# Three experts with 64 slots loaded ahead of the routing, and 32 slots for the 14 emptiest

## The chip, the cores and the metric

The kernel runs on one core of a Trainium2 chip. The metric is device time in microseconds, as the median of the runs shown; a run is one launch of the whole layer. TensorE (PE) does the matrix products, VectorE (DVE) and ScalarE (ACT) the elementwise work, GpSimd (POOL) issues the gathers and scatters, and SyncE (SP) issues nearly all other transfers. Transfers of SP go through one queue in the order in which SP issues them, and SP waits in that order too.

## The reference

One residual layer on 512 tokens of 1024 channels, float32. First a mixer: a norm, one projection, a gated convolution branch and a spatial gating branch, and an output projection. Then a mixture of 32 experts in 4 groups, of which this change speaks:

```python
g_sel = jnp.argmax(g_logits, axis=-1)                      # one group of 4 for each token
e_logits = jnp.take_along_axis(e_logits, g_sel[:, None, None], axis=1)[:, 0]
top_v, top_i = lax.top_k(e_logits, TOP_K)                  # two of its 8 experts
e_w = jax.nn.softmax(top_v, axis=-1) * g_w
expert_id = g_sel[:, None] * EXPERTS_PER_GROUP + top_i
...
def run_block(args):                                       # SwiGLU, 1024 -> 512 -> 1024
    xb, e = args
    return (jax.nn.silu(xb @ w_gate[e]) * (xb @ w_up[e])) @ w_down[e]
...
y = y_pad[dest] * sorted_w[:, None].astype(h.dtype)
out = jnp.zeros((n_tok, d), h.dtype).at[sorted_tok].add(y)
```

A final norm follows. 512 tokens with two experts each make 1024 assignments over 32 experts. How they fall depends on the data. With the inputs of the reference (seed 0), experts 0, 1 and 2 get 16, 22 and 10 of them. The other 29, sorted by their counts, get 115, 113, 97, 88, 58, 55, 51, 36, 36, 32, 32, 31, 27, 26, 26, 20, 18, 16, 16, 15, 15, 11, 10, 10, 9, 4, 3, 3, 3.

## The kernel before

The mixer takes the first 457 us or so. It is split matmul work with its own weights, and it holds the on-chip memory that the experts' weights need afterwards. The router's logits are made token block by token block with the last matmuls of the mixer (`out_mm`, `out_tr`, `out_logits`, `route_norm`, `route_sel`, `route_rank`, `route_tab`), and the normed tokens are written to `h2d` in HBM by POOL (`h2_out`).

**Ranks.** After the last block the experts are sorted by their number of tokens, on the chip (`krow`, `kcol`, `kr`, `Pm`), and the sorted list of expert numbers, `eid`, is what SP reads to know which weights to load. The first `NS` places are an exception: they are experts 0 to `NS`-1 by number, whatever their counts (`kre` and `kce` hold the offsets that put them first). Since their numbers are known, their weights can be loaded before the routing is done.

**Slots.** Each rank has a fixed number of token slots: 128 for ranks below `NBIG`, 64 for those above. A last check (`capr`, `over`) compares the counts with the slots; if one does not fit, the branch `overflow` runs at the end and does the rest in `NOV` more blocks. With 128 slots an expert's gate and up products go to two PSUM tiles; with 64 slots they share one, gate in partitions 64 to 127 and up in 0 to 63, as column halves of the PE array.

**Order.** `order` lists the ranks as they are computed: the `NS` first, then as the string `ORDER` says (`s` the next of 64 slots, `b` the next of 128). Position n in that order is what the loops count.

**Weights.** An expert has three pieces of 2 MB: two of gate and up (`(n, 0)` and `(n, 1)`) and one of down (`(n, 2)`). The list `loads` is the order in which they go through SP's queue. `piece()` issues the next one. It goes to one of nine buffers (`SLOTS`, tags w0 to w8, taken in turn from `rot`) and waits for three things: that the buffer's last reader is done, that the load two places earlier has landed (`throttle`, `DEEP` is 2), and, from rank `NS` on, for `eid`. Loads are counted from 0 in what follows; loads 0 to 3·`NS`-1 are those of the experts that come first by number. Near the end of the list stand the last expert but one, then the two halves `Y` of the scattered results `yd` (2 MB each), then the three pieces of the last expert. The buffers lie where the mixer's tiles lay, so the first ones come free only as the mixer ends.

**One position n of the loop**, in PE's order: gate and up products with the two pieces (`up`), the transposes of the next position's tokens (`x_tr`, which also issues the gather of position n+4), the down products of position n-1 (`down`), the transposes of this position's hidden values (`h_tr`). `glu` on ACT and DVE lies between. `down` copies its result to `ysb` and POOL scatters it to `yd` by an indirect transfer; each scatter waits for the one before it to land, and what POOL has to do after it waits too. With 64 slots a token's row of 1024 is scattered as two half rows, from partitions 0 to 63 and 64 to 127. A gather moves `cap[r]` rows and a scatter of 64 slots `64 + cap[r]`, where `cap` also takes the bound 1024 / (r - NS + 1) on how many tokens rank r can hold, so the late ranks' transfers have numbers of rows such as 53, 46 or 37.

**The end.** The last three positions are not scattered but added on the chip (`late_down`, `late_add`, `late_x`). The `Y` loads read `yd`, so they wait for the last scatter, that of position 28. Then the rows are summed, normed and written, and the last expert's rows go out through one indirect transfer.

Of the kernel before, what the change touches and what calls it, by code (L numbers as in the profile page):

```python
# [8 lines left out]
F32 = mybir.dt.float32  # L9
FR = mybir.dt.float32r  # L10
I32 = mybir.dt.int32
F16 = mybir.dt.float16
# [9 lines left out]
NS, NBIG, DEEP, NLATE, LATE_AT = 2, 8, 2, 3, -16  # L22
NOV = 9
# [3 lines left out]
ORDER = "ssb" * 6 + "s" * 12  # L27
# [54 lines left out]
def body(tc, nc, d, out, dbg=None):  # L82
# [116 lines left out]
    pool.memset(capr[:, :NBIG], 128.0)  # L199
    pool.memset(capr[:, NBIG:], 64.0)  # L200
# [536 lines left out]
    cap = [128] * NS + [min(128 if r < NBIG else 64, 2 * T // (r - NS + 1)) for r in range(NS, NE)]  # L737
    order, bs_, ss_ = list(range(NS)), list(range(NS, NBIG)), list(range(NBIG, NE))
    for c in ORDER:
        order.append((bs_ if c == "b" else ss_).pop(0))  # L740
# [94 lines left out]
    def slots(p, n, gi_, si_):  # L835
# [21 lines left out]
    slots(tab[:, :NS], NS, gi[:, :NS], si[:, :NS])  # L857
# [39 lines left out]
    def x_tr(n):  # L897
        if n >= NE:
            return
        m = 128 if order[n] < NBIG else 64  # L900
        xg = XG[n % len(XG)]
        XT[n] = xT = m1.tile([128, KT, m], F32, name="xT", tag=("xh", "xl")[n % 2])
        nb = m * KT // 512
        kb = KT // nb
        for hf in range(nb):
            p = aux()
            for k in range(kb):
                kk = hf * kb + k
                pe.transpose(p[:, k * m:(k + 1) * m], xg[:m, kk * 128:(kk + 1) * 128], ident[:m, :m])  # L909
            pv = p.rearrange("p (k t) -> p k t", k=kb)  # L910
            ks = slice(hf * kb, hf * kb + kb)
            dve.tensor_tensor(xT[:, ks], pv, bc(gfp[:, ks], m), ALU.mult)
        gather(n + len(XG))

    def up(n, c):
        small = order[n] >= NBIG
        if c == 0:
            E[n] = {}
            p = acc()
            E[n]["g"], E[n]["u"] = (p[64:128], p[:64]) if small else (p, acc())  # L920
        w = W[n, c].rearrange("p (q k f) -> p q k f", q=2, k=4)
        for kk in range(4):
            kt = c * 4 + kk
            for q in range(2):
                pe.matmul(E[n]["gu"[q]], XT[n][:, kt], w[:, q, kk], start=kt == 0, stop=kt == KT - 1,  # L925
                          skip_group_check=True)

    def glu(n):
        m = 128 if order[n] < NBIG else 64
        s_ = m2.tile([128, DE], F32, name="sg", tag="sg")[:m]  # L930
        act.activation(s_, E[n]["g"], AF.Silu)  # L931
        E[n]["h"] = h = m2.tile([128, DE], F32, name="h", tag="h")[:m]
# [5 lines left out]
    def h_tr(n):  # L938
        m = 128 if order[n] < NBIG else 64
        p = acc()  # L940
        for k in range(4):
            pe.transpose(p[:, k * m:(k + 1) * m], E[n]["h"][:, k * 128:(k + 1) * 128], ident[:m, :m])
        hh = m2.tile([128, 4, m], F32, name="hh", tag="hh")
        act.activation(hh, p[:, :4 * m].rearrange("p (k t) -> p k t", k=4), AF.Copy)
# [10 lines left out]

    def down(n):
        small = order[n] >= NBIG
# [186 lines left out]
    def overflow():  # L1144
# [20 lines left out]
        dve.tensor_scalar(ce, ce, 64.0, None, ALU.add)  # L1165
# [130 lines left out]
```

## Time and profile before

| | |
|---|---|
| median of 3 runs | 1016.41 us (1015.29 to 1018.13) |
| the profiled execution | 1016.92 us, its span 1015.1 us |
| mean granted clock of PE | 0.973 |
| PE busy | 945.5 us, 93% of the span |
| DVE, ACT, POOL busy | 395.1, 225.7, 112.5 us |
| read from HBM, written | 260.06 MB, 17.97 MB |
| last matmul of the mixer | starts 454.17 us and runs in a group of 12 for 3.02 us |
| first matmul of an expert | 480.77 us |
| last weights issued | 984.9 us |

The rest of the profile is given by time from the span's start. A row of the timeline has the start, the duration, the engine, the line, the operation, the tiles that it writes and reads, how many such instructions in a row, and in brackets how long the engine sat idle before it and what ended that. `SPq` rows are issues of transfers: they last 0.33 us where they stand alone, and one row with several has the time from the first issue to the end of the last. A matmul of float32 is two instructions in the trace, so the 16 products of `up(n, c)` with 128 slots show as 16 instructions for 8 in the program.

### The profile page before, as it was taken

Reading aid. Unit: us, or ns where it says so; the run is one execution under the profiler, and the core shown is the slowest. Engines: PE = TensorE matmul, PEld = TensorE weight load, DVE = VectorE, ACT = ScalarE, POOL = GpSimd, SP = SyncE. Lnnn points to the kernel's source line nnn. Section 1 sums busy time; section 2 is a strip of 40 time slices with the busy share of each in tenths; the row PEclk is TensorE's granted clock in tenths of the full one; section 3 lists DMA queues with packets and bytes.
Section 4 is the critical chain, followed back from the end, with each engine's and each line's share of the span. In section 5 each row is a group of like instructions: output and inputs, shape, how many; then the busy total and the mean of one; then the engine's idle time right before and its main releaser. Section 6 shows DMA issues by size and latency. Waiting matters only on the chain. (4 is left out here: it accounts for less than half of the span.)

```text
span 1015.1 us, 10676 instructions
## 1 busy us (share of the span) xinstructions
PE 945.5 (93%) x4210; PEld 558.4 (55%) x4210; DVE 395.1 (39%) x662; ACT 225.7 (22%) x317; POOL 112.5 (11%) x102
## 2 busy tenths in 40 slices
PE   8999999999999999993999999999999998787774
PEld 6867588888778888883444443434444333232221
DVE  7697758889447534247111101110111111022053
ACT  6302223433237323232100101111100010110123
POOL 3300000000000000503011111111101021111010
PEclk9999999999999999996999999999999999999978
DMA  5558312322221333953989999999999999999794
GB/s 221 193 156 291 116 55 83 111 80 88 96 83 41 130 119 105 414 206 145 355 323 409 409 411 412 415 405 405 418 404 398 390 394 374 408 410 410 298 355 154
DMA packets 42536, 271.38 MB, mean 267 GB/s; under 512 B 12776, under 2 KB 15976, under 8 KB 25970
## 3 DMA queue, kind: packets, MB, share of 16 engines
q1 hardware_dynamic: 31680, 260.14, 65.8%
q0 software_dynamic: 10800, 10.51, 3.1%
q8 instruction: 35, 0.57, 0.2%
q14 instruction: 19, 0.16, 0.0%
q10 hardware_dynamic: 2, 0.00, 0.0%
HBM read 260.06 MB, written 17.97 MB: 274 GB/s over the span
## 5 line engine op out<-in xcount | busy, mean ns | idle before, releaser
L925 PE MATMUL acc<-w,xT 128*64 128x512 f32 (+1 forms) x1024 | 291.0, 609 | 18.0 <-DMA w<-in_wexp 18.0
L350 PE MATMUL acc<-hT,hl 128*128 128x512 f32 x912 | 210.5, 390 | 0.0
L925 PEld LDWEIGHTS acc<-w,xT 128*64 128x64 f32 (+1 forms) x1024 | 103.7, 153 | 182.4 <-issue 163.2
L350 PEld LDWEIGHTS acc<-hT,hl 128*128 128x128 f32 x912 | 170.7, 188 | 37.4 <-issue 1.9
L936 DVE TENSOR_TENSOR h<-sg,acc 64x512 f32<-64x512 f32 (+1 forms) x31 | 21.1, 681 | 364.8 <-ACT sg L931 252.3
L953 PE MATMUL acc<-w,hh 128*64 128x512 f32 (+1 forms) x512 | 146.3, 604 | 8.9 <-DMA w<-in_wexp 6.0
L156 DVE TENSOR_TENSOR hl<-f,hl 128x2048 fp32r<-128x2048 f32 (+1 forms) x36 | 80.2, 2229 | 78.9 <-ACT hl L146 78.8
L340 DVE SCALAR_TENSOR_TENSOR cv<-cv,cs,cv 128x500 f32<-128x500 f32 (+19 forms) x150 | 103.7, 741 | 0.8
L953 PEld LDWEIGHTS acc<-w,hh 128*64 128x64 f32 (+1 forms) x512 | 51.2, 151 | 80.2 <-issue 70.2
L146 ACT ACTIVATE hl<-f 128x2048 fp32r<-128x2048 f32 x35 | 66.8, 1911 | 46.8 <-issue 29.2
L931 ACT ACTIVATE sg<-acc 64x512 f32<-64x512 f32 (+1 forms) x32 | 19.0, 595 | 253.4 <-PE acc L925 253.4
L972 POOL DMA_INDIRECT yd<-ysb,si x29 | 33.6, 1159 | 255.2 <-DMA yd<-ysb,si 95.1
L853 POOL DMA_INDIRECT xg<-h2d,gi x32 | 33.2, 1037 | 170.9 <-PE aux L909 161.3
L358 PE MATMUL acc<-hl,mT 128*128 128x512 f32 x192 | 46.6, 396 | 0.0
L601 POOL TENSOR_TENSOR X<-X,rbo 128x1024 f32<-128x1024 f32 x4 | 9.4, 2394 | 329.2 <-DMA X<-in_x 329.2
L350 PE MATMUL acc<-sT,hl 128*128 128x512 f32 x192 | 45.1, 394 | 0.0
L350 PE MATMUL acc<-yT,hl 128*128 128x512 f32 x192 | 44.2, 389 | 0.0
L358 PE MATMUL acc<-hl,hT 128*128 128x512 f32 x192 | 43.8, 390 | 0.0
L350 PEld LDWEIGHTS acc<-sT,hl 128*128 128x128 f32 x192 | 36.0, 188 | 8.4 <-issue 1.0
L358 PEld LDWEIGHTS acc<-hl,hT 128*128 128x128 f32 x192 | 36.0, 188 | 8.3 <-issue 0.8
L350 PEld LDWEIGHTS acc<-yT,hl 128*128 128x128 f32 x192 | 36.0, 188 | 7.5
L358 PEld LDWEIGHTS acc<-hl,mT 128*128 128x128 f32 x192 | 35.3, 188 | 7.2
(261 smaller groups left out, 625.4 us busy)
## 6 DMA issues: line engine op xcount, KB each, us to landing
w<-in_wexp SPq DMA_DIRECT2D x93, 2048.0 KB, 10.6
f<-in_wmix SPq DMA_DIRECT2D x36, 1024.0 KB, 4.8
yd<-z SPq DMA_DIRECT2D x1, 4096.0 KB
w<-yd SPq DMA_DIRECT2D x2, 2048.0 KB, 14.0
w<-in_wexp SPq DMA_DIRECT2D x8, 512.0 KB, 13.5
xs<-in_x SPq DMA_DIRECT2D x4, 512.0 KB, 6.2
X<-in_x SPq DMA_DIRECT2D x4, 512.0 KB, 4.4
h2d<-h POOLq DMA_DIRECT2D x4, 512.0 KB, 2.9
```

Of the source, the lines that this page charges most:

```text
L146: act.activation(HI[i], src, AF.Copy)
L156: dve.tensor_tensor(LO[i][:, :n], src[:, :n], h[:, :n], ALU.subtract)
L340: dve.scalar_tensor_tensor(cY[:, j, s_:], cA[:, j, :T - s_], cw(j, t), cY[:, j, s_:], ALU.mult, ALU.add)
L350: pe.matmul(p, w[:, k], mv[m][:, k], start=n == 0, stop=n == 3 * KT - 1)
L358: pe.matmul(p, mv[m][:, kh * 4 + k, bs], w[:, k], start=kh + n == 0, stop=kh == 1 and n == 11)
L601: pool.tensor_tensor(X2[:, :, cs_], X2[:, :, cs_], rbo[:, cs_].unsqueeze(1).to_broadcast([128, NB, 256]), ALU.add)
L853: pool.indirect_dma_start(out=XG[n % len(XG)][:m], out_offset=None, in_=h2d, in_offset=bass.IndirectOffsetOnAxis(ap=gi[:m, r:r + 1], axis= ...
L925: pe.matmul(E[n]["gu"[q]], XT[n][:, kt], w[:, q, kk], start=kt == 0, stop=kt == KT - 1, skip_group_check=True)
L931: act.activation(s_, E[n]["g"], AF.Silu)
L936: dve.tensor_tensor(h, s_, E[n]["u"], ALU.mult)
L953: pe.matmul(y[hf], E[n]["hT"][:, kt], w[:, kt, hf * 512:hf * 512 + 512], start=first and kt == 0, stop=kt == 3, skip_group_check=True)
L972: pool.indirect_dma_start(out=ydh if small else yd, out_offset=bass.IndirectOffsetOnAxis(ap=si[:m, r:r + 1], axis=0), in_=ysb[:m], in_offs ...
```

## The change

- `NS` goes from 2 to 3, and those three get 64 slots each where the two had 128. All nine buffers are filled by loads 0 to 8, in the same places, and the rotation `rot` starts with the buffers in the order in which they are used; the ninth comes into it at load 19.
- `NMID` is 18: ranks 3 to 7 have 128 slots (five where there were six beside the first two), ranks 8 to 17 have 64 (ten, where there were 24), and ranks 18 to 31 have 32 (14).
- An expert with 32 slots uses the four column quarters of the PE array, each with 256 of the 512 columns: gate and up each as two half widths (`up`), and the down product as four quarters of the row (`down_tiny`). The scatter then moves quarter rows of 1 KB, from all 128 partitions. Its gather moves 32 rows. `t` in `ORDER` stands for it.
- With `NS` 3 the bound in `cap` is never the smaller one, so every gather has 32, 64 or 128 rows and every scatter 128.
- The offsets, capacities and the tables of slots follow (`kre`, `kce`, `capr`, `qt4`, `tT`, `pt`, `si`, `ce`); `overflow` may have up to 15 blocks.

```diff
-NS, NBIG, DEEP, NLATE, LATE_AT = 2, 8, 2, 3, -16
-NOV = 9
+NS, NBIG, DEEP, NLATE, LATE_AT = 3, 8, 2, 3, -16
+NOV, NMID = 15, 18
+ORDER = "tsb" * 5 + "t" * 9 + "s" * 5
...
-ORDER = "ssb" * 6 + "s" * 12
...
-    pool.memset(capr[:, :NBIG], 128.0)
-    pool.memset(capr[:, NBIG:], 64.0)
+    pool.memset(capr[:, :NS], 64.0)
+    pool.memset(capr[:, NS:NBIG], 128.0)
+    pool.memset(capr[:, NBIG:NMID], 64.0)
+    pool.memset(capr[:, NMID:], 32.0)
...
-    cap = [128] * NS + [min(128 if r < NBIG else 64, 2 * T // (r - NS + 1)) for r in range(NS, NE)]
+    cap = [64] * NS + [min(128 if r < NBIG else 64 if r < NMID else 32, 2 * T // (r - NS + 1)) for r in range(NS, NE)]
...
-    loads = [(0, 0), (0, 1), (1, 0), (1, 1), (0, 2), (1, 2), (2, 0), (2, 1)]
-    for n in range(3, NE):
+    loads = [(0, 0), (0, 1), (1, 0), (1, 1), (0, 2), (2, 0), (2, 1), (1, 2), (2, 2), (3, 0), (3, 1)]
+    for n in range(4, NE):
         loads += [(n, 0), (n, 1), (n - 1, 2)]
...
-    rot, tag_of = [SLOTS[k] for k in (0, 1, 2, 3, 4, 6, 7, 5, 8)], {}
+    rot, tag_of = list(SLOTS[:-1]), {}
...
+            if k == NSLOT + 10:
+                rot.insert(0, SLOTS[-1])
...
-    slots(tab[:, :NS], NS, gi[:, :NS], si[:, :NS])
+    slots(tab[:, :NS], NS, gi[:, :NS], None)
...
-    tb1 = slots(pt[:, NS:NE], NE - NS, gi[:, NS:], None)
-    dve.tensor_copy(si[:, NS:NBIG], tb1[:, :NBIG - NS])
-    dve.tensor_scalar(si[:, NBIG:], tb1[:, NBIG - NS:], 2.0, hf01, ALU.mult, ALU.add)
+    tb1 = slots(pt[:, :NE], NE, gi[:, NS:], None, NS)
+    dve.tensor_copy(si[:, NS:NBIG], tb1[:, NS:NBIG])
+    for c0, c1, mul, off in ((0, NS, 2.0, hf01), (NBIG, NMID, 2.0, hf01), (NMID, NE, 4.0, qt4)):
+        dve.tensor_scalar(si[:, c0:c1], tb1[:, c0:c1], mul, off, ALU.mult, ALU.add)
...
+            if tiny:
+                for i in range(4):
+                    f = i % 2 * 256
+                    pe.matmul(E[n]["p"][i * 32:i * 32 + 32, :256], XT[n][:, kt], w[:, 1 - i // 2, kk, f:f + 256],
+                              start=kt == 0, stop=kt == KT - 1, skip_group_check=True)
+                continue
...
+    ydq = yd.rearrange("t (h c) -> (t h) c", h=4)
+
+    def down_tiny(n):
+        r = order[n]
+        w = W[n, 2].rearrange("p (k f) -> p k f", k=4)
+        p = acc()
+        for kt in range(4):
+            f = kt // 2 * 32
+            for i in range(4):
+                pe.matmul(p[i * 32:i * 32 + 32, :256], E[n]["hT"][:, kt % 2, f:f + 32], w[:, kt, i * 256:i * 256 + 256],
+                          start=kt == 0, stop=kt == 3, skip_group_check=True)
+        ysb = m1.tile([128, 256], F32, name="ysb", tag="ysb", bufs=2)
+        act.activation(ysb, p[:, :256], AF.Copy)
+        pool.indirect_dma_start(out=ydq, out_offset=bass.IndirectOffsetOnAxis(ap=si[:, r:r + 1], axis=0),
+                                in_=ysb, in_offset=None, bounds_check=8 * T - 1, oob_is_err=False)
```

SP's queue where the weights begin, before (`w0` to `w10` are loads 0 to 10, the number behind them is the program's own; TENSOR_LOAD is SP's read of `eid`, which waits for the routing):

```order
L792 DMA w0_3171<-in_wexp 128x4096
L792 DMA w1_3173<-in_wexp 128x4096
L792 DMA w2_3174<-in_wexp 128x4096
L792 DMA w3_3175<-in_wexp 128x4096
L792 DMA w4_3184<-in_wexp 128x4096
L792 DMA w5_3170<-in_wexp 128x4096
L795 TENSOR_LOAD eid_3256
L803 ISA
L803 DMA w6_3176<-in_wexp 128x4096
```

and now:

```order
L801 DMA w0_3177<-in_wexp 128x4096
L801 DMA w1_3179<-in_wexp 128x4096
L801 DMA w2_3180<-in_wexp 128x4096
L801 DMA w3_3181<-in_wexp 128x4096
L801 DMA w4_3190<-in_wexp 128x4096
L801 DMA w5_3176<-in_wexp 128x4096
L801 DMA w6_3182<-in_wexp 128x4096
L801 DMA w7_3189<-in_wexp 128x4096
L801 DMA w8_3178<-in_wexp 128x4096
L804 TENSOR_LOAD eid_3265
L812 ISA
L812 DMA w9_3365<-in_wexp 128x4096
```

Loads 6, 7 and 8 stood behind the read of `eid` and now stand ahead of it; load 9 is the first behind it.

PE's queue where the experts begin, before (the first sizes are the output's; `xT` is the transposed tokens, `hh` the transposed hidden values; L925 is gate and up, L953 down):

```order
L925 MATMUL acc<-w_3171,xT 128x512 x8
L925 MATMUL acc<-w_3173,xT 128x512 x8
L909 MATMUL aux<-ident,xg_3178 128x128 x8
L942 MATMUL acc<-ident,h 128x128 x4
L925 MATMUL acc<-w_3174,xT 128x512 x8
L925 MATMUL acc<-w_3175,xT 128x512 x8
L909 MATMUL aux<-ident,xg_3292 128x64 x8
L953 MATMUL acc<-w_3184,hh 128x512 x8
```

and now, from the same place up to the first expert of 32 slots (L944 gate and up, L974 down, L940 gate and up of 32 slots):

```order
L944 MATMUL acc<-w_3177,xT 64x512 x8
L944 MATMUL acc<-w_3179,xT 64x512 x8
L922 MATMUL aux<-ident,xg_3184 128x64 x8
L963 MATMUL acc<-ident,h 128x64 x4
L944 MATMUL acc<-w_3180,xT 64x512 x8
L944 MATMUL acc<-w_3181,xT 64x512 x8
L922 MATMUL aux<-ident,xg_3304 128x64 x8
L974 MATMUL acc<-w_3190,hh 64x512 x8
...
L940 MATMUL acc<-w_3365,xT 32x256 x16
L940 MATMUL acc<-w_3378,xT 32x256 x16
```

The first two experts' products now pair up in the column halves as those of 64 slots did; with 32 slots there are twice as many matmuls, each of half the width, in four quarters.

POOL's queue late in the experts, before (`xg` are gathers, with their rows; `yd` the scatters, whose row count the program does not print here):

```order
L853 DMA xg1_3178<-h2d_74,gi_3254 42x1024
L972 DMA yd_75<-ysb_4724,si_3255 1024x1024
L853 DMA xg2_3292<-h2d_74,gi_3254 40x1024
L972 DMA yd_75<-ysb_4790,si_3255 2048x512
L853 DMA xg3_3293<-h2d_74,gi_3254 39x1024
L972 DMA yd_75<-ysb_4855,si_3255 2048x512
L853 DMA xg0_3177<-h2d_74,gi_3254 37x1024
L972 DMA yd_75<-ysb_4920,si_3255 2048x512
```

and now:

```order
L862 DMA xg0_3183<-h2d_74,gi_3263 32x1024
L990 DMA yd_75<-ysb_4799,si_3264 4096x256
L862 DMA xg1_3184<-h2d_74,gi_3263 32x1024
L990 DMA yd_75<-ysb_4886,si_3264 4096x256
L862 DMA xg2_3304<-h2d_74,gi_3263 32x1024
L990 DMA yd_75<-ysb_4973,si_3264 4096x256
L862 DMA xg3_3305<-h2d_74,gi_3263 64x1024
L990 DMA yd_75<-ysb_5060,si_3264 4096x256
```

Gathers and scatters alternate as they did; their rows are 32 or 64 where they were 42, 40, 39 and 37, and the scatters (L990) write quarter rows.

More of the change, by code (lines that the diff above doesn't have):

```diff
@@ L198, in body @@
     capr = keep.tile([128, NE], F32, name="capr")
-    pool.memset(capr[:, :NBIG], 128.0)
-    pool.memset(capr[:, NBIG:], 64.0)
+    pool.memset(capr[:, :NS], 64.0)
+    pool.memset(capr[:, NS:NBIG], 128.0)
+    pool.memset(capr[:, NBIG:NMID], 64.0)
+    pool.memset(capr[:, NMID:], 32.0)
+    qt4 = keep.tile([128, 1], F32, name="qt4")
+    dve.tensor_scalar(qt4, vali[:, 0:1], 32.5, None, ALU.is_ge)
+    for q in (64.5, 96.5):
+        dve.scalar_tensor_tensor(qt4, vali[:, 0:1], q, qt4, ALU.is_ge, ALU.add)
     gp = [aux(), aux()]
@@ L833, in sm, with slots @@
         return v
-    def slots(p, n, gi_, si_):
+    def slots(p, n, gi_, si_, o=0):
         tb = sm([3, n])
@@ L899, in x_tr @@
             return
-        m = 128 if order[n] < NBIG else 64
+        m = rows_(order[n])
         xg = XG[n % len(XG)]
         XT[n] = xT = m1.tile([128, KT, m], F32, name="xT", tag=("xh", "xl")[n % 2])
-        nb = m * KT // 512
+        nb = max(1, m * KT // 512)
         kb = KT // nb
@@ L915, in up @@
     def up(n, c):
-        small = order[n] >= NBIG
+        small, tiny = rows_(order[n]) < 128, order[n] >= NMID
         if c == 0:
             E[n] = {}
-            p = acc()
-            E[n]["g"], E[n]["u"] = (p[64:128], p[:64]) if small else (p, acc())
+            p = E[n]["p"] = acc()
+            E[n]["g"], E[n]["u"] = (p[64:128, :256 if tiny else DE], p[:64, :256 if tiny else DE]) if small else (p, acc())
         w = W[n, c].rearrange("p (q k f) -> p q k f", q=2, k=4)
@@ L928, in glu @@
     def glu(n):
-        m = 128 if order[n] < NBIG else 64
-        s_ = m2.tile([128, DE], F32, name="sg", tag="sg")[:m]
+        m = max(64, rows_(order[n]))
+        fw = 256 if order[n] >= NMID else DE
+        s_ = m2.tile([128, DE], F32, name="sg", tag="sg")[:m, :fw]
         act.activation(s_, E[n]["g"], AF.Silu)
-        E[n]["h"] = h = m2.tile([128, DE], F32, name="h", tag="h")[:m]
+        E[n]["h"] = h = m2.tile([128, DE], F32, name="h", tag="h")[:m, :fw]
         if n == NE - 1:
@@ L938, in h_tr @@
     def h_tr(n):
-        m = 128 if order[n] < NBIG else 64
+        m = max(64, rows_(order[n]))
+        nk = 2 if order[n] >= NMID else 4
         p = acc()
-        for k in range(4):
+        for k in range(nk):
             pe.transpose(p[:, k * m:(k + 1) * m], E[n]["h"][:, k * 128:(k + 1) * 128], ident[:m, :m])
-        hh = m2.tile([128, 4, m], F32, name="hh", tag="hh")
-        act.activation(hh, p[:, :4 * m].rearrange("p (k t) -> p k t", k=4), AF.Copy)
+        hh = m2.tile([128, nk, m], F32, name="hh", tag="hh")
+        act.activation(hh, p[:, :nk * m].rearrange("p (k t) -> p k t", k=nk), AF.Copy)
         E[n]["hT"] = hh
@@ L954, in down_mm @@
                           stop=kt == 3, skip_group_check=True)
+    ydq = yd.rearrange("t (h c) -> (t h) c", h=4)
[12 more added lines that the diff above has]
+                                in_=ysb, in_offset=None, bounds_check=8 * T - 1, oob_is_err=False)
     def down(n):
-        small = order[n] >= NBIG
+        small = rows_(order[n]) < 128
+        if order[n] >= NMID:
+            down_tiny(n)
+            return
         p = acc()
```

37 lines of the change are left out of this document (23 added, 14 removed).

## The prediction

> **What bounds the kernel now.** I read the windows first, for who is busy in which stretch, with the columns us, busy time (and instructions) of PE, PE's weight loads, DVE, ACT and POOL, then granted clock, DMA share and GB/s.
>
> ```profile
> 450.00:476.00 26.00, 12.87 (x77) 10.08 (x75) 19.08 (x100) 7.58 (x13) 5.95 (x8) 0.74 0.22 82
> 476.00:530.00 54.00, 50.28 (x154) 23.09 (x155) 8.89 (x30) 5.28 (x9) 7.39 (x8) 0.90 0.91 341
> 530.00:730.00 200.00, 200.00 (x786) 80.94 (x788) 23.94 (x38) 20.90 (x39) 26.87 (x27) 1.00 1.01 410
> 730.00:950.00 220.00, 198.16 (x896) 76.82 (x894) 27.79 (x49) 23.52 (x47) 30.39 (x27) 0.99 1.00 399
> 950.00:968.00 18.00, 13.60 (x60) 4.77 (x57) 1.28 (x2) 3.34 (x6) 2.21 (x1) 0.91 0.52 192
> 968.00:996.00 28.00, 20.83 (x60) 6.97 (x58) 18.53 (x23) 9.18 (x14) 3.27 (x1) 0.76 0.97 373
> ```
>
> From 530 to 950 two things read as full, PE and the DMA engines. Which one sets the pace is told by SP's issues, from the timeline.
>
> ```profile
> 442.09 0.33 SPq L792 DMA_DIRECT2D w<-in_wexp  x1
> 474.42 0.97 SPq L803 DMA_DIRECT2D w<-in_wexp  x2
> ...
> 490.78 7.19 SPq L803 DMA_DIRECT2D w<-in_wexp  x2
> ...
> 541.77 349.88 SPq L803 DMA_DIRECT2D w<-in_wexp  x65
> ...
> 896.71 52.82 SPq L803 DMA_DIRECT2D w<-in_wexp  x11
> 965.28 0.94 SPq L788 DMA_DIRECT2D w<-yd  x2
> ```
>
> and, of all loads of L803:
>
> ```profile
> DMA to landing us min/median/max: 8.7/10.7/17.6
> ```
>
> Loads 17 to 92 start at 541.77 and the last at 949.2 (896.71 + 52.82 - 0.33), 5.43 us apart. Two are allowed in flight and one takes 10.7 us from issue to landing (the last row, the median), twice 5.35. So a load goes out when the one two places earlier lands, not when PE frees a buffer, and 2.1 MB in 5.43 us beside the gathers and scatters is all that the DMA engines carry. That stretch is set by DMA; PE is nearly as long, which its groups by shape show:
>
> ```profile
> L925 PE MATMUL acc<-w,xT 128*64 128x512 f32 x768 | 176.2, 609 | 18.0 <-DMA w<-in_wexp 18.0
> ...
> L925 PE MATMUL acc<-w,xT 128*128 128x512 f32 x256 | 114.8, 607 | 0.0
> L953 PE MATMUL acc<-w,hh 128*64 128x512 f32 x384 | 89.2, 606 | 8.9 <-DMA w<-in_wexp 6.0 <-ACT hh L944 2.9
> ...
> L953 PE MATMUL acc<-w,hh 128*128 128x512 f32 x128 | 57.1, 599 | 0.0
> ...
> L329 PE MATMUL acc<-ct 128*32 128x512 f32 x192 | 22.9, 593 | 0.1
> L909 PE MATMUL aux<-ident,xg 64*128 64x64 f32 x192 | 17.0, 229 | 0.0
> ...
> L942 PE MATMUL acc<-ident,h 64*128 64x64 f32 x96 | 11.0, 235 | 1.0 <-DVE h L934 1.0
> ```
>
> The busy time is a union, so pairs in column halves count once. An expert of 64 slots (24 of them) costs (176.2 + 89.2 + 17.0 + 11.0)/24 = 12.2 us with its transposes (L909, L942). One of 128 (8 of them) costs (114.8 + 57.1)/8 = 21.5, with some 2 of transposes 23.5. `ssb` is then 47.9 us of PE against 3·3·5.43 = 48.9 of DMA.
>
> So time can be had only where the DMA engines are not full: 450 to 530, and 950 to 968.
>
> **The change part by part.** *The 14 of 32 slots.* The nearest row is L329, four column quarters of 512: 192 instructions in 22.9 us, 0.48 us for a group of four. At 256 columns I take half, 0.24. Gate and up are 64 instructions (16 groups, 3.8 us), down 32 (8 groups, 1.9), with transposes 6.7 us in place of 12.2. If the quarters did not overlap it would be four times 5.7, near 23.5. I take 6.7, as the row has the same shape but for the width. `tsb` is then 42.4 us of PE, `t` 6.7 of 16.3: PE gets faster where DMA sets the pace, worth nothing. It would be the other way round only from 13.2 us for a `t` on (48.9 - 12.2 - 23.5).
>
> *Loads 6 to 8 ahead of the routing.* They waited for `eid` until 474.42. Load 6 now goes out behind load 5 (442.09), and 7 and 8 as the mixer's last matmul gives up their buffers, at 457.2.
>
> ```profile
> 454.17 3.02 PE L358 MATMUL acc<-hl,mT 128*128 128x512 f32 x12
> ...
> 464.72 0.53 POOL L718 DMA_DIRECT2D h2d<-h  x1 [4.17 <-DVE scr L704]
> ...
> 473.24 1.08 POOL L853 DMA_INDIRECT xg<-h2d,gi  x1 [6.14 <-DVE padsg L874]
> ...
> 480.64 0.20 PE L992 MATMUL acc<-padsg 32*128 32x32 f16 x1 [1.91 <-DVE padsg L991]
> 480.77 2.08 PE L925 MATMUL acc<-w,xT 128*128 128x512 f32 x2
> ```
>
> ```profile
> h2d<-h POOLq DMA_DIRECT2D x4, 512.0 KB, 2.9
> ```
>
> They land by about 470, in time that was 0.22 busy. In their way stand the last write of `h2d` (464.72) and behind it the first gather (473.24). Alone the write takes 2.9 us (the row of the page's transfers); under load, at the 10.7 of the weights, it would end at 475.4 and cost the first gather 2 us. The price is 0 to 2; I take 0.5. The first matmul (480.77) waits for DVE's chain through L991, which has two more small operations of `si` and one less for `xT`: about as before.
>
> *When load 9 starts.* It needs the buffer of (0, 0). Before it went out at 490.78, when the 16 instructions from 480.77 were through, 10.0 us. Now half as many steps do it. An even half is 5.0, but the earlier half ran while the clock was still low (0.90 over that window), so I take 6.2: load 9 at 487.5 with the 0.5 above. Alone it takes 8.7 us and lands at 496.2. The next buffers come free faster than a load lands: an expert of 64 slots passes its three in 12.2 us, against 16.3. So from load 10 the 5.43 holds, load 15 lands at 496.2 + 6·5.43 = 528.8, and load 17 goes out then in place of 541.77: **13.0 us earlier**. Bounds: 11 with the full 2 us and a slower first half, 15.5 if load 9 goes out at 486.
>
> *The end.* DMA is idle for 0.48·18 = 8.6 us between load 92 and the `Y` loads. These rows show why:
>
> ```profile
> 584.33 1.00 POOL L972 DMA_INDIRECT yd<-ysb,si  x1 [7.26 <-ACT hh L944]
> ...
> 729.16 1.64 POOL L853 DMA_INDIRECT xg<-h2d,gi  x1 [6.21 <-PE aux L909]
> ...
> 934.06 2.25 POOL L972 DMA_INDIRECT yd<-ysb,si  x1 [8.58 <-DMA yd<-ysb,si]
> ...
> 942.84 0.60 ACT L966 ACTIVATE ysb<-acc 128x512 f32<-128x512 f32 x1 [4.33 <-PE acc L953]
> ...
> 960.34 2.21 POOL L972 DMA_INDIRECT yd<-ysb,si  x1 [24.04 <-DMA yd<-ysb,si]
> ...
> 974.65 1.28 DVE L1063 SCALAR_TENSOR_TENSOR X<-w,wt,X 128x1024 f32<-128x1024 f32 x1 [19.93 <-DMA w<-yd]
> ```
>
> and, of all scatters of L972:
>
> ```profile
> DMA to landing us min/median/max: 7.4/10.2/33.2
> ```
>
> The last scatter's data is ready at 943.4, but the scatter is issued at 960.34, as the one before it, issued at 934.06, takes 25 us to land; `Y` waits for it until 965.28. The scatters (last row) take 10.2 us as a rule and 33.2 at worst. Slow ones are long on POOL too: 2.25 and 2.21 us for 103 and 101 rows, 1.64 for the gather of 53, against 1.00 for 128. The last two scatters now have 128 rows, and 26 tokens each where they had 9 and 4. At 10.2 us the last lands at 953.6 on the old clock, and the `Y` loads queue behind load 92, which lands at 949.2 + 10.7 = 959.9. The first `Y` lands 5.4 later, at 965.3, in place of 974.6. What follows, weights and DVE's sums, starts from there. **9 us earlier**, between 0 (a last scatter over 16.5 us) and 9.5.
>
> The trace leaves it open whether those transfers are slow for their row counts or for their many empty slots. [...]
>
> *The rate.* 730 to 950 ran at 399 GB/s against 410. At 410 its 220 us would be 6 shorter. [...] Between 0 and 6 I take 2.
>
> *The rest*: three small DVE operations and two memsets in the first microseconds, beside the load of x: nothing, and 0.5 us without that cover.
>
> **Sum**: 1016.9 (the profiled execution, 1.8 beyond its span) - 13.0 - 9 - 2 = 992.9, and 0.5 less against the median of the runs: **992 us**.
>
> **Rivals.** *The hole before `Y` stays*, since 14 scatters of quarter rows, mostly empty, hold up POOL's queue until the last is late: 1003. For it: scatters wait for each other, 24.04 us in the row above. Against: five experts of 64 slots follow the `t`s, with 16 us between scatters.
>
> *The early loads gain nothing*, since they crowd out `h2d` and the first gather as much as they bring: 1005. For it speaks the 17.6 at worst of a load; against, that the DMA is 0.22 busy there.
>
> *PE becomes the bound*, slower than before: the quarters do not overlap, `t` takes 23.5, `tsb` 59.2. That is 10.3 us too much five times and 7.2 nine times, 116, less some 15 in hand (nine buffers are three experts' weights, and one of those, 16.3 us, is a margin): near 1093. It decides from 13.2 us for a `t`. L329's 593 ns each in 22.9 together speaks against.
>
> *PE cools down.* With a `t` PE works some 2 us of each 5.43 and rests over 3. In 450:476, with PE half busy, the granted clock was 0.74; in 730:950, 90% busy, 0.99. `tsb` keeps PE 87% busy. Only under 0.87 does it outlast DMA; at 0.75 it takes 56.5, five times 7.6 less the 15: 1015, no gain. [...]
>
> *The slots do not suffice and the overflow branch runs*: nine blocks or more of 6.3 MB at 410 GB/s, 15 us each, beyond 1130. With 22, 115, 55 and 20 tokens at most for the four sizes the reference's own counts fit.
>
> **How the numbers follow.** Chances: forecast 0.72 (its own range 985 to 998), the hole 0.13, no early gain 0.06, the bound on PE 0.04, the cool PE 0.04, overflow 0.01. The range for 8 in 10 reaches over the forecast's bounds to the next two cases: 985 to 1005. A measurement here tells 0.3% (3 us) from no change. Forecast, hole and no early gain are faster, 0.91; a cool PE is the same, with a part slower: 0.03 and 0.01; the bound and overflow are slower: 0.06 in all.
>
> **What would show it.** Loads 7 and 8 issued at about 457, load 9 at 486 to 489; DMA share near 1 from 490 to the end, with no hole between load 92 and `Y`; the last scatter issued when its data is there and landed in some 10 us; POOL's indirect transfers all near 1.0 us; a `t` of 6 to 8 us on PE, which waits for weights all the way. Wrong if PE is full in `tsb`, if the granted clock falls below 0.87 there, or if a load waits for PE after load 12.

## The result

The changed kernel takes 992.31 us (median of 4 runs, 991.05 to 993.35) against 1016.62 us of the kernel before beside it (4 runs, 1015.29 to 1018.13): **0.976 of the time before, 95% interval 0.974 to 0.978**. Its profiled execution took 992.66 us with a span of 990.7; before it was 1016.92 and 1015.1. Forecast were 992 us, with 985 to 1005 as the range.

The windows of the changed kernel, with the same columns as before (us, then busy time of PE, weight loads, DVE, ACT and POOL, then granted clock, DMA share and GB/s):

```profile
476.00:530.00 54.00, 48.97 (x291) 18.85 (x293) 9.36 (x32) 6.75 (x14) 11.88 (x13) 0.92 0.84 327
530.00:730.00 200.00, 183.50 (x974) 81.26 (x971) 20.31 (x35) 18.98 (x39) 25.62 (x26) 0.96 1.00 406
730.00:926.00 196.00, 135.95 (x1191) 64.80 (x1189) 20.13 (x44) 15.89 (x40) 22.29 (x23) 0.84 1.00 408
926.00:944.00 18.00, 13.65 (x72) 5.15 (x70) 1.28 (x2) 3.03 (x6) 0.98 (x1) 1.00 1.00 416
944.00:972.00 28.00, 23.32 (x84) 7.61 (x82) 21.34 (x25) 12.23 (x19) 3.28 (x1) 0.95 0.97 373
```

PE, which was as full as the DMA engines, is now 92% busy in the first stretch and 69% in the second, and its granted clock falls to 0.84 there, as a mean over the stretch. The DMA engines stay full up to 972; the stretch that was half empty before (950:968, share 0.52) has no successor. SP's issues, from the timeline (start, length, how many):

```profile
453.10 4.89 SPq L801 DMA_DIRECT2D w<-in_wexp  x2
...
486.02 390.14 SPq L812 DMA_DIRECT2D w<-in_wexp  x73
...
528.67 0.33 SPq L812 DMA_DIRECT2D w<-in_wexp  x1
...
932.85 0.33 SPq L812 DMA_DIRECT2D w<-in_wexp  x1
935.90 0.94 SPq L797 DMA_DIRECT2D w<-yd  x2
```

Loads 7 and 8 go out at 453.1 and 457.7 (453.10 + 4.89 - 0.33; 457 was forecast for both), load 9 at 486.02, load 17 at 528.67, the last of the full stretch, load 92, at 932.85, and the loads of `Y` 3 us behind it. Before, those times were 490.78 (load 9), 541.77, 949.2 and 965.28. What SP waited for is told by the chart of waits (us in total, times, the longest):

```profile
SPq L812 <- DMA w<-in_wexp: 390.3, 86, 6.3
...
SPq L812 <- PE acc L944: 17.4, 5, 11.1
...
SPq L797 <- DMA yd<-ysb,si: 2.6, 1, 2.6
```

A load waits for an earlier load 86 times. Of the five waits for gate and up products (L944), four are those of loads 9 to 12 (11.1, 2.8, 2.7 and 0.5 us); behind load 12 no load of the full stretch waits for PE, at any line, for more than 0.4 us. `Y` waits 2.6 us for the last scatter. The scatters at the end, POOL's timeline, and the landings of all scatters of that line:

```profile
912.05 1.11 POOL L1012 DMA_INDIRECT yd<-ysb,si  x1 [15.68 <-ACT hh L965]
927.46 0.98 POOL L1012 DMA_INDIRECT yd<-ysb,si  x1 [14.30 <-ACT hh L965]
...
979.36 0.99 POOL L1179 DMA_INDIRECT out<-o,cs  x1 [17.66 <-DVE o L1178]
```

```profile
DMA to landing us min/median/max: 7.6/8.4/11.9
```

Both wait for ACT's data and no longer for the scatter ahead of them. The last one is issued at 927.46 in place of 960.34, and the final write of `out` at 979.36 in place of 1004.51.

### The profile page after: what moved, and what is told of

The parts are those of the page before. It is cut to its first block, busy times and chain, and to the rows that moved or that the text cites. A ratio compares the mean times of both kernels' runs of the same rounds, so it can differ in the third digit from the quotient of the medians.

```text
span 990.7 us, 11957 instructions
## 1 busy us (share of the span) xinstructions
PE 867.6 (88%) x4856; PEld 543.8 (55%) x4856; DVE 384.2 (39%) x660; ACT 218.4 (22%) x317; POOL 106.6 (11%) x104
## 5 line engine op out<-in xcount | busy, mean ns | idle before, releaser
L944 PE MATMUL acc<-w,xT 128*64 128x512 f32 (+1 forms) x576 | 169.2, 615 | 17.4 <-DMA w<-in_wexp 17.3
L956 DVE TENSOR_TENSOR h<-sg,acc 64x256 f32<-64x256 f32 (+2 forms) x31 | 17.4, 560 | 356.2 <-ACT sg L951 274.5
L944 PEld LDWEIGHTS acc<-w,xT 128*64 128x64 f32 (+1 forms) x576 | 60.4, 156 | 113.1 <-issue 98.2
L974 PE MATMUL acc<-w,hh 128*64 128x512 f32 (+1 forms) x288 | 92.8, 637 | 16.1 <-DMA w<-in_wexp 14.8
L940 PE MATMUL acc<-w,xT 128*32 128x256 f32 x896 | 66.5, 452 | 35.3 <-DMA w<-in_wexp 35.3
L951 ACT ACTIVATE sg<-acc 64x256 f32<-64x256 f32 (+2 forms) x32 | 16.0, 501 | 250.8 <-PE acc L944 155.8
L974 PEld LDWEIGHTS acc<-w,hh 128*64 128x64 f32 (+1 forms) x288 | 32.9, 165 | 63.4 <-issue 59.3
L940 PEld LDWEIGHTS acc<-w,xT 128*32 128x32 f32 x896 | 32.1, 126 | 63.8 <-issue 28.5
L862 POOL DMA_INDIRECT xg<-h2d,gi x32 | 30.6, 956 | 211.4 <-PE aux L922 203.9
L986 PE MATMUL acc<-w,hh 128*32 128x256 f32 x448 | 33.5, 450 | 13.3 <-DMA w<-in_wexp 13.3
## 6 DMA issues: line engine op xcount, KB each, us to landing
w<-in_wexp SPq DMA_DIRECT2D x93, 2048.0 KB, 10.6
h2d<-h POOLq DMA_DIRECT2D x4, 512.0 KB, 10.3
```

Source lines behind the costliest of these rows:

```text
L862: pool.indirect_dma_start(out=XG[n % len(XG)][:m], out_offset=None, in_=h2d, in_offset=bass.IndirectOffsetOnAxis(ap=gi[:m, r:r + 1], axis= ...
L940: pe.matmul(E[n]["p"][i * 32:i * 32 + 32, :256], XT[n][:, kt], w[:, 1 - i // 2, kk, f:f + 256], start=kt == 0, stop=kt == KT - 1, skip_gro ...
L956: dve.tensor_tensor(h, s_, E[n]["u"], ALU.mult)
L974: pe.matmul(y[hf], E[n]["hT"][:, kt], w[:, kt, hf * 512:hf * 512 + 512], start=first and kt == 0, stop=kt == 3, skip_group_check=True)
L986: pe.matmul(p[i * 32:i * 32 + 32, :256], E[n]["hT"][:, kt % 2, f:f + 32], w[:, kt, i * 256:i * 256 + 256], start=kt == 0, stop=kt == 3, sk ...
```

## The experiments

Each run is told with its time over that of the kernel before on the same chip, with its 95% interval. Load 9 is the first that waits for a buffer of an expert, load 17 the first of the full stretch, load 92 the last before `Y`; the times are those of SP's issues, in us from the start of the span. The kernel before was slower on the chip of the first four runs (1018.96 us) than beside the others (1016.6 to 1017.3), so those four are compared by their ratios and with each other.

| run | over before | load 9 | load 17 | load 92 | Y |
|---|---|---|---|---|---|
| before | 1 | 490.78 | 541.77 | 949.2 | 965.28 |
| the change | 0.976 (0.974 to 0.978) | 486.02 | 528.67 | 932.85 | 935.90 |
| loads 6 to 8 late | 0.981 (0.978 to 0.984) | 490.92 | 537.64 | 941.64 | 944.77 |
| first two with 128 slots | 0.988 (0.985 to 0.991) | 490.73 | 541.84 | 946.29 | 949.47 |
| no 32 slots | 0.974 (0.970 to 0.978) | 484.94 | 529.43 | 933.70 | 936.37 |
| before, even rows | 0.984 (0.981 to 0.987) | 492.11 | 542.53 | 943.51 | 946.51 |
| the change again | 0.976 (0.974 to 0.979) | 486.12 | 528.57 | 932.99 | 935.78 |
| odd rows at the end | 0.993 (0.990 to 0.995) | 484.49 | 528.70 | 934.36 | 958.26 |
| first three with 32 | 0.971 (0.969 to 0.973) | 481.54 | 525.52 | 926.38 | 929.36 |

### Loads 6 to 8 behind the routing

```
-        if r < NS:
+        if k < 6:
             throttle(sp.dma_start(W[n, q], wexp[r, q]))
...
-    for _ in range(3 * NS):
+    for _ in range(6):
         piece()
...
-    for _ in range(NSLOT - 3 * NS):
+    for _ in range(NSLOT - 6):
         piece()
```

> The changed kernel, but loads 6, 7 and 8 wait for the routing again; the first three experts keep 64 slots. The theory: both halves of the step are needed, and without the early loads the DMA engines run without a stop from 474.4 us, but carry three loads more. In the kernel before, load 7 landed at 490.67 with nothing in its way but DMA; load 9 can go out then, and eight loads at 5.43 us later load 17 goes out at 534, 5.4 us later than in the changed kernel (528.67): about 997.5 us. A rival gives the early loads all 13 us: load 17 at 541.8, 1005 us. Another gives it all to the slots: load 17 at 529, 992 us.

SP's issues and the window behind the routing in this run:

```profile
475.41 409.18 SPq L812 DMA_DIRECT2D w<-in_wexp  x76
...
537.64 0.33 SPq L812 DMA_DIRECT2D w<-in_wexp  x1
```

```profile
476.00:530.00 54.00, 48.57 (x291) 18.77 (x293) 9.61 (x33) 6.76 (x14) 12.20 (x13) 0.92 1.01 385
```

The DMA engines are full from the routing on (1.01), no load waits for PE between 476 and 545 us, and still load 17 goes out at 537.64: 4.1 us earlier than before and 9.0 later than in the changed kernel, between the 534 of the theory and the 541.8 of the rival. The expectation failed in its pace: loads 9 to 17 took (537.64 - 490.92)/8 = 5.84 us each and not 5.43, in a window that moved 385 GB/s; why no more, these runs do not show. In time it is 0.981, some 9 us behind the run without 32 slots on the same chip (999.9 against 990.62).

### The early loads, but 128 slots for the first two

```
-    pe.matmul(pt[:, :NS], tT[:, 1], Pm[:, :NS], start=True, stop=True)
+    pe.matmul(pt[:, :2], tT[:, 0], Pm[:, :2], start=True, stop=True)
+    pe.matmul(pt[:, 2:3], tT[:, 1], Pm[:, 2:3], start=True, stop=True)
...
-    cap = [64] * NS + [
+    cap = [128, 128, 64] + [
...
-    rows_ = lambda r: 64 if r < NS else 128 if
+    rows_ = lambda r: 64 if r == 2 else 128 if
```

> The changed kernel with its nine early loads, but the first two experts have 128 slots again, the third 64, as before. The theory: TensorE passes buffers on no sooner than before (loads 12 and 13 went out at 514.13 and 521.83 for its sake), so the early loads are worth nothing by themselves: load 9 at about 490, load 17 at 540 to 542, 1004 to 1006 us. The rival, that the early loads bring their part whatever the slots: load 17 at 536 or before, 1000 us or less.

```profile
490.73 7.21 SPq L812 DMA_DIRECT2D w<-in_wexp  x2
...
541.84 0.33 SPq L812 DMA_DIRECT2D w<-in_wexp  x1
```

and the window in which the loads wait for PE:

```profile
490.00:540.00 50.00, 48.98 (x202) 22.22 (x204) 5.57 (x9) 5.84 (x9) 4.92 (x5) 1.00 0.82 307
```

Load 9 and load 17 stand where they stood before the change, to 0.1 us. PE is busy 49 of 50 us while the DMA engines have 18% to spare: three loads more in the buffers bring nothing if PE hands the buffers on no sooner. So the early loads alone are worth 0 of the 13.1 us, the smaller slots alone 4.1, and both together 13.1. Each half removes one of two limits, and the time comes only when both are gone.

### No 32 slots

```
-    pool.memset(capr[:, NBIG:NMID], 64.0)
-    pool.memset(capr[:, NMID:], 32.0)
+    pool.memset(capr[:, NBIG:], 64.0)
...
-    rows_ = lambda r: 64 if r < NS else 128 if r < NBIG else 64 if r < NMID else 32
+    rows_ = lambda r: 64 if r < NS else 128 if r < NBIG else 64
...
-        small, tiny = rows_(order[n]) < 128, order[n] >= NMID
+        small, tiny = rows_(order[n]) < 128, False
```

> The changed kernel, but the 14 emptiest experts have 64 slots and half rows; each scatter of a small expert has 128 rows, each gather 64. The theory: DMA sets the pace from 490 us on (5.39 us for a load) and an expert of 64 slots (12.2 us of TensorE against 16.2 of DMA) hides as well as one of 32: 992 us within 2, load 92 at 933 within 1.5. The rival, that TensorE's shorter work is behind the better rate of the second half: load 92 at 936 or later, 995 us or more.

```profile
730.00:930.00 200.00, 167.58 (x797) 63.64 (x797) 24.76 (x44) 21.06 (x42) 23.12 (x24) 0.98 1.00 408
```

PE is busy 167.58 of 200 us here and the DMA engines move the same 408 GB/s. Load 92 goes out at 933.70, 0.85 us later than in the changed kernel, and the time is 0.974 (0.970 to 0.978) against 0.976 (0.974 to 0.978). The 32 slots, the largest part of the diff, are worth nothing that these runs can tell.

### The kernel before, with even row counts

```
-    cap = [128] * NS + [min(128 if r < NBIG else 64, 2 * T // (r - NS + 1)) for r in range(NS, NE)]
+    cap = [128] * NBIG + [64] * (NE - NBIG)
```

> The kernel before, with one edit: each gather has 64 or 128 rows and each scatter 128, where many had 99 to 127 (or 35 to 60) by the bound on the tokens of a rank. The theory: transfers of 103, 101 and 53 rows were slow for their row count, so the hole before the loads of Y goes: the last scatter lands some 9 us earlier, and the rate of the second half rises from 399 to about 408 GB/s, up to 3 us more: 1004 to 1008 us. The rival, that they were slow for their empty slots: the last scatters still take about 25 us, 1016 us. A second rival, that the rate was held down by TensorE: the hole goes but load 92 stays at 949, 1007 us.

The landings of all scatters of L972 in this run, then POOL's timeline at the end:

```profile
DMA to landing us min/median/max: 6.5/8.3/11.5
```

```profile
923.11 0.99 POOL L972 DMA_INDIRECT yd<-ysb,si  x1 [13.99 <-ACT hh L944]
938.11 0.98 POOL L972 DMA_INDIRECT yd<-ysb,si  x1 [14.01 <-ACT hh L944]
```

```profile
530.00:730.00 200.00, 200.00 (x792) 81.35 (x792) 23.39 (x37) 21.42 (x40) 26.15 (x27) 1.00 1.00 410
730.00:940.00 210.00, 193.84 (x888) 75.52 (x886) 28.35 (x50) 23.84 (x47) 26.85 (x28) 1.00 1.01 411
```

The slots are as empty as before (the last two scatters hold 9 and 4 tokens), and no scatter takes more than 11.5 us where the worst took 33.2. Emptiness falls. (That worst one had 128 rows itself; it was issued at 734.78, behind the gather of 53 rows at 729.16, which took 35.2 us to land.) `Y` goes out 3 us behind load 92, and the second half runs at 411 GB/s with PE 92% busy, so neither PE nor the number of bytes held it at 399: loads 17 to 92 took (943.51 - 542.53)/75 = 5.346 us each instead of 5.432, which is 6.4 us over the stretch. The ratio of 0.984 is 16 us, more than the 8 to 12 expected: the rate was worth twice what I had allowed it. One line of the old kernel's table of row counts holds two thirds as much time as the whole change gained.

The trace of the kernel before could have told the two theories apart ahead of any run, since its scatters have many row counts. On POOL's timeline there, those of 117, 108 and 106 rows:

```profile
833.64 1.03 POOL L972 DMA_INDIRECT yd<-ysb,si  x1 [9.12 <-DMA yd<-ysb,si]
...
891.38 1.03 POOL L972 DMA_INDIRECT yd<-ysb,si  x1 [6.15 <-DMA yd<-ysb,si]
901.04 1.62 POOL L972 DMA_INDIRECT yd<-ysb,si  x1 [7.18 <-DMA yd<-ysb,si]
```

They landed after 9.4, 8.7 and 22.1 us. The last two hold 10 tokens each, so it is not the empty slots; and 117 is odd and quick, 106 even and slow, so "odd" and "even" in the names of these runs are no more than names.

### Odd rows for the last two scatters

Beside this run the changed kernel ran once more, as a measure.

> The changed kernel once more, as the measure for the three runs beside it on the same chip. Every theory expects what was measured: 0.976 of the time before, load 9 at 486 and load 17 at 528.7 us, load 92 at 933.

It did: 992.71 us and 0.976 (0.974 to 0.979). The edit to it:

```
-        m = 64 + cap[r] if small else cap[r]
+        m = 64 + {27: 39, 28: 37}.get(n, cap[r]) if small else cap[r]
```

> The changed kernel, but the last two scatters have 103 and 101 rows, as before the change, instead of 128; the rows left out are empty slots. They are issued at 912 and 927.5 us. The theory (slow for the row count): POOL spends about 2.2 us on each, the first lands 25 us after its issue, at 937, the second goes out then and lands at 945 to 955, and the loads of Y with it rather than at 935.9: the hole is back in part, 4 to 15 us later than the changed kernel, my estimate 8. The rival (slow for empty slots) expects no difference: there are fewer empty slots than in the changed kernel.

POOL's and SP's timelines, and the landings of L1012:

```profile
912.82 2.27 POOL L1012 DMA_INDIRECT yd<-ysb,si  x1 [15.69 <-ACT hh L965]
947.56 2.21 POOL L1012 DMA_INDIRECT yd<-ysb,si  x1 [32.48 <-DMA yd<-ysb,si]
```

```profile
958.26 0.94 SPq L797 DMA_DIRECT2D w<-yd  x2
```

```profile
DMA to landing us min/median/max: 8.0/9.5/33.8
```

Two scatters with 103 and 101 rows in place of 128, each with fewer rows, cost 16.2 us (1008.95 against 992.71): two thirds of all that the change gained. The mechanism is the expected one, with a larger price. The first, at 912.82, takes 33.8 us beside the loads; the second waits for it on POOL until 947.56, and `Y` for the second until 958.26. I had taken 25 us for a landing, from before, and 15 us at most for the whole. The second, issued when the weights before `Y` had landed (the DMA engines moved 27 GB/s or less from 942.6 to 948), took only 10.6 us to land, so the long landing is paid beside a full queue of weights. What the queue of POOL carries from 912 to 948 differs; first the run with odd rows, then the changed kernel, with the packets and MB of that queue:

```profile
q0 software_dynamic: 848, 0.14, 2.2%
```

```profile
q0 software_dynamic: 160, 0.26, 1.9%
```

One scatter of 103 rows makes 848 packets, where two of 128 rows make 160 and move nearly twice the bytes. Which row counts are slow beside the loads, the runs show by the landings alone: 33.8 us here and 25.4 in the kernel before for 103 rows, 22.1 for 106, 9.4 and 8.7 for 117 and 108, and at most 11.5 for 128 with even rows. Why, and which engine carried a packet, these rows do not show.

### 32 slots for the first three as well, and two variants

```
-    pool.memset(capr[:, :NS], 64.0)
+    pool.memset(capr[:, :NS], 32.0)
...
-    cap = [64] * NS + [
+    cap = [32] * NS + [
...
-    rows_ = lambda r: 64 if r < NS else
+    rows_ = lambda r: 32 if r < NS else
```

> The changed kernel, but the first three experts have 32 slots too (they hold 16, 22 and 10 tokens). If the start of load 9 still sets the end, as in the theory, it goes out when half as many TensorE instructions are through: 482 to 484 us instead of 486.0, and the whole ends 2 to 4 us earlier, 0.973 of the time before. The rival: the first loads after the routing are held by the gathers and not by the buffer, and load 17 stays at 528 to 529 us: no difference.

```profile
481.54 2.89 SPq L812 DMA_DIRECT2D w<-in_wexp  x2
...
525.52 0.33 SPq L812 DMA_DIRECT2D w<-in_wexp  x1
```

986.99 us, 0.971 (0.969 to 0.973): faster than the changed kernel beside it (992.71). Load 9 goes out 4.6 us earlier, load 17 3.1, load 92 6.6 (926.38 against 932.99). So the start gives 3.1 us, and the rest comes from a pace of 5.345 us a load in place of 5.392, which I did not expect and cannot explain by the slots of the first three. Of the 4.6 us of load 9 up to 1.6 need not be the edit's: with odd rows at the end, in a kernel that does the same as the changed one up to there, load 9 went out at 484.49.

The second variant gives only the first three 32 slots, the 14 emptiest 64, and writes the small operations of the rest of the routing behind the first sixteen matmuls; the third has 32 slots throughout with those operations moved:

```
     x_tr(0)
-    route_rest()
...
             piece()
+            if n == c == 0:
+                route_rest()
```

> The first three experts have 32 slots, the 14 emptiest have 64 again (as in the run without 32 slots), and the small operations of the rest of the routing, for which the first matmul of an expert waited at 479.86 us, are written behind that expert's first sixteen. If load 9 sets the end: it goes out at 480 to 482 us, 4 to 6 us earlier than in the changed kernel, and the time is 0.970 to 0.972 of that before. If the 32 slots of the 14 emptiest are worth something after all, it ends later than the run with 32 slots throughout.

> 32 slots for the first three experts and for the 14 emptiest, with the small operations of the rest of the routing written behind the first sixteen matmuls. If the start of load 9 sets the end: up to 1 us earlier than the run with 32 slots for the first three alone, 0.970 of the time before. If those operations were hidden anyway, the same as that run, 0.971.

They took 987.83 us, 0.971 (0.968 to 0.973), with load 9 at 481.63 and load 17 at 526.55, and 989.2 us, 0.971 (0.969 to 0.974), with load 9 at 482.41 and load 17 at 528.33. The moved operations are worth nothing that these runs can tell, as if they had been hidden. The 32 slots of the 14 emptiest are worth nothing here either. And load 9 is not all that sets load 17: in the third variant it went out 3.7 us earlier than in the changed kernel, and load 17 within 0.4 us of it.

### Three loads in flight

```
-NS, NBIG, DEEP, NLATE, LATE_AT = 3, 8, 2, 3, -16
+NS, NBIG, DEEP, NLATE, LATE_AT = 3, 8, 3, 3, -16
```

> The changed kernel with three loads of weights in flight in place of two. The theory says that the DMA engines are full with two (their share reads 1.00 from 530 us on): a load then takes some 16 us from issue to landing instead of 10.7, the pace stays at 5.35 to 5.40 us a load, and the time within 3 us of the changed kernel. The rival, that two in flight set the pace: 5.3 us a load or less, 985 us or less. A third: the scatters and gathers get a smaller share and the last ones land late, 995 us or more.

The windows, and the landings of the loads of L812:

```profile
530.00:730.00 200.00, 181.04 (x976) 80.35 (x973) 20.31 (x35) 19.01 (x39) 25.71 (x27) 0.97 1.01 415
730.00:920.00 190.00, 132.41 (x1182) 63.26 (x1180) 18.87 (x42) 15.74 (x40) 22.20 (x23) 0.86 1.01 412
```

```profile
DMA to landing us min/median/max: 7.5/15.8/19.7
```

A load takes 15.8 us, as the theory said, and the same DMA share now carries 415 and 412 GB/s in place of 406 and 408. The loads land hardly faster: from load 17 to load 92 one lands every 5.33 us, where it was 5.37 in the changed kernel and 5.35 with 32 slots for the first three. The time is 988.36 us, 0.971 (0.969 to 0.973), a gain of some 4 us that lies between the theory and the rival; in the profile load 92 lands 2.1 us earlier (940.58 against 942.71), and the rest is not traced. `Y` goes out at 933.43, 7.8 us behind load 92 instead of 3, since load 92 now goes out a place earlier and the last scatter ends last.

With 32 slots for the first three as well:

> Both edits that gained: the first three experts with 32 slots, and three loads in flight. If the two gains are separate (an earlier start, and a rate of 412 to 415 GB/s in place of 406), they add: 0.966 to 0.969 of the time before. If both are the same gain (DMA busy sooner after the routing): 0.971, as each alone.

987.01 us, 0.971 (0.968 to 0.973): the gains do not add in the times, though the windows show the higher rate (414 and 413 GB/s) and the profiled span was the shortest of all, 982.6. Load 92 lands at 936.24 here and at 936.25 with two in flight and the same slots, and `Y` goes out at 929.37 and 929.36: by the landings, the third load in flight brought nothing on top. Five kernels stand at 0.971, below the changed kernel's 0.976, one of them with an interval that ends where its own begins (0.974); which of the five is best these runs do not tell.

## Why the prediction was right

**When load 9 starts** (-13.0): the mechanism right, the number right by luck. Load 17 went out at 528.67 (528.8 forecast), 13.1 us earlier than before, but the steps to it were off and cancelled. These rows are from the page's transfers (the median of four writes) and from the timelines of POOL and PE:

```profile
h2d<-h POOLq DMA_DIRECT2D x4, 512.0 KB, 10.3
```

```profile
473.89 0.99 POOL L862 DMA_INDIRECT xg<-h2d,gi  x1 [6.35 <-DVE padsg L883]
```

```profile
479.99 9.42 PE L944 MATMUL acc<-w,xT 128*64 128x512 f32 x32
```

Under load the writes of `h2d` landed after 10.3 us instead of 2.9, the last of them after 6.5, and the first gather went out 0.65 us later than before (473.24). That cost nothing behind it: the first product of an expert started 0.8 us earlier than before (480.77), where 0.5 had been added. Load 9 went out at 486.02 (487.5 forecast) and landed after 7.6 us and not 8.7, at 493.6. The six landings from there to load 15, which lets load 17 go, then took 34.9 us where six times 5.43 is 32.6. So load 9 landed 2.6 us earlier than forecast, and the six behind it lost 2.3 again. The step "from load 10 the 5.43 holds" failed, but not for want of buffers: loads 11 and 12 still waited for PE, 2.7 and 0.5 us, but from 490 to 530 the DMA engines were full (1.01). In these 35 us the gathers and scatters held 9.5% of them, against 7.5% from 600 to 635; whether that is the whole reason is open.

The working gives the 13.0 to early loads and slots as one chain, and the runs show that it is one: 0 and 4.1 us apart. Load 17 follows load 9 only in part: from the issue of load 9 to that of load 17 a load took 5.33 us in the changed kernel, and 5.84 and 5.50 in kernels that differ little.

**The end** (-9): right in that the last two scatters, now of 128 rows, land sooner, and larger than its bound of 9.5. That the last of them would land after 10.2 us was the author's estimate, the median of all scatters before; the last one landed after 8.4 us. The first `Y` is added here, on DVE's timeline:

```profile
947.85 1.28 DVE L1103 SCALAR_TENSOR_TENSOR X<-w,wt,X 128x1024 f32<-128x1024 f32 x1 [9.47 <-DMA w<-yd]
```

That is 26.8 us earlier than before (974.65), of which load 92 brings 16.35; the other 10.45 are the hole. Odd rows in two scatters bring it back (`Y` at 958.26), even rows in the kernel before take it away (946.51), and the empty slots are in both. The scatters of 32 slots, the emptiest of all, landed after 6.2 to 7.7 us. One detail of the working was wrong: the last two scatters now hold 32 and 31 tokens, not 26 each (63 rows of 4 KB are the 0.26 MB above).

**The rate** (-2, bounds 0 to 6): right in sign, an incomplete sum; the 2 was the author's estimate, between nothing and the 6 us of 410 GB/s. Loads 17 to 92 took 5.389 us each in place of 5.432, 3.2 us together. With even rows the kernel before gains 6.4 us there, all of it in the second half (from load 54 on); the changed kernel gains 4.3 us in the second half and loses 1.0 in the first. Why it falls short of the even rows is open. The 406 GB/s in place of 410 in the first half tell less than they seem to: from 530 to 730 SP's queue moved 76.45 MB where it had moved 76.68, and the gathers and scatters, now with fewer rows, 4.62 instead of 5.29. The run without 32 slots has the same pace (5.39), so the quarter rows of 1 KB are not the reason.

**The sum** had nothing for what is given back at the end. The final write came 25.15 us earlier, where 13.1 + 3.2 + 10.45 make 26.75. That write and the last matmuls on the timelines of POOL and PE, first before (the write in the changed kernel stands above), then the matmuls in the changed kernel:

```profile
996.38 1.08 PE L1119 MATMUL acc<-X,w 128*64 128x512 f32 x4
997.29 3.60 PE L953 MATMUL acc<-w,hh 128*64 128x512 f32 x16
...
1004.51 1.01 POOL L1139 DMA_INDIRECT out<-o,cs  x1 [16.01 <-DVE o L1138]
```

```profile
969.68 1.98 PE L1159 MATMUL acc<-X,w 128*64 128x512 f32 x4
...
971.45 4.29 PE L974 MATMUL acc<-w,hh 128*64 128x512 f32 x16
```

The same twenty matmuls took 0.90 and 0.69 us longer, which is the missing 1.6. The granted clock was 1.00 over both rows before and 0.50 and 0.84 over them now: the cool PE of one of the rivals, in a place where nothing hides it. Some 0.75 us more went behind the final write (the span is 24.4 us shorter); its cause is open. So the hole and the rate brought 2.65 us more than forecast, the end of the kernel gave 2.35 back, and that the total meets the forecast to a few tenths of a microsecond is luck too.

**The 32 slots** (worth nothing): right, with a `t` that cost more than its 6.7 us. The groups by shape:

```profile
L940 PE MATMUL acc<-w,xT 128*32 128x256 f32 x896 | 66.5, 452 | 35.3 <-DMA w<-in_wexp 35.3
...
L986 PE MATMUL acc<-w,hh 128*32 128x256 f32 x448 | 33.5, 450 | 13.3 <-DMA w<-in_wexp 13.3
...
L922 PE MATMUL aux<-ident,xg 32*128 32x32 f32 x112 | 9.9, 229 | 0.0
```

Gate, up and down took (66.5 + 33.5)/14 = 7.1 us where 5.7 had been taken, 0.30 us for a group of four and not 0.24; with the transposes of x (9.9/14) it is 7.8, and some more with those of h. That is a mean over two clocks, as PE's timeline shows:

```profile
763.49 1.94 PE L986 MATMUL acc<-w,hh 128*32 128x256 f32 x32 [0.51 <-DMA w<-in_wexp]
...
769.48 3.64 PE L940 MATMUL acc<-w,xT 128*32 128x256 f32 x32 [3.79 <-DMA w<-in_wexp]
```

Both are eight groups of four. The first, at a granted clock of 1.00, took 1.94 us, 0.24 for a group, so "at 256 columns I take half" held; the second, at 0.50, took 3.64. Of the 42 such bursts 13 took 2.9 to 3.6 us, all from 769 us on, where one `t` follows another; why those and not the others, the runs do not show. The term that failed is the clock of a `t`, for which the working took full speed. It decides nothing: the margin went up to 13.2.

**The rivals.** That the hole stays because of empty slots is refuted twice. That the early loads gain nothing is true of them alone, for another reason than the one given: buffers, not crowding. PE did cool below 0.87 as a mean (0.84 from 730 to 926), and to half the clock in single bursts (0.50), but behind `tsb`, where a `t` has time to spare; the 0.96 in 530:730 is where it would have counted. The quarters overlap (0.24 us for a group of four at a clock of 1.00), and no overflow ran.

## What to carry to other kernels

Where a transfer's row count comes out of a formula, look up in the trace how long each count takes to land, and round it up to one that lands soon (64 or 128 here), even if that writes empty rows: beside the weights 103 rows landed after 25.4 and 33.8 us, three to four times the 8.4 of the changed kernel's scatters of 128, and the price is paid by whatever waits on the same queue (`Y` went out at 958.26 and not at 935.78). Where two limits lie over each other, an early transfer and a late buffer, neither edit alone shows what it is worth (0 and 4.1 of 13.1 us here); take both away before judging one. An engine that becomes idle beside the bound gains nothing by it (0.976 with the 32 slots, 0.974 without), and here PE ran twenty of the last matmuls at a granted clock of 0.50 and 0.84 in place of 1.00, 1.6 us longer.

## What was not expected of the hardware

A DMA share of 1.00 does not tell the rate. Beside shares of 1.00 and 1.01 stood 399 GB/s in the second stretch of the kernel before, 406 and 408 in the changed kernel, 410 and 411 with even rows and 415 and 412 with three loads in flight. "All that the DMA engines carry" in the prediction, a load in 5.43 us, was short by 1 to 2%: with two in flight the same loads also went at 5.35 to 5.39.

The pace of the loads comes in two groups: 5.39 us in the changed kernel and in those with late loads, with 128 slots for the first two and without 32 slots; 5.35 in the kernel before with even rows and in two of the three with 32 slots for the first three (5.37 in the third). Both occur on the same chip. The cause stays open; it is worth some 3 us.

The speed of PE in the first experts differs between kernels that do the same there. The second expert's gate and up, first in the second run of the changed kernel, then in the one with odd rows at the end:

```profile
492.86 7.09 PE L944 MATMUL acc<-w,xT 128*64 128x512 f32 x32
```

```profile
491.25 9.91 PE L944 MATMUL acc<-w,xT 128*64 128x512 f32 x32
```

The same 32 matmuls take 7.09 or 9.91 us, after a rest of 2.11 us in both, 0.72 of the speed in the second. With odd rows the buffers come free later for it, and of the 1.6 us by which load 9 went out earlier nothing is left at load 17 (528.70 against 528.57). Why the speed differs is open.
